# First feed-forward block: the snapshot of one product in PSUM, half of a low part on VectorE, and a fixed order of products

## The chip, the cores and the metric

The kernel runs on one core of one Trainium2 chip. The metric is the device time of one execution in microseconds. Three executions of the kernel before took 986.99, 991.24 and 991.29 us, so the median is 991.24 us. A separate execution was profiled; it took 986.47 us, and its profiled span is 984.5 us.

## The reference

One inference step of a decoder trunk of depth one: 512 prompt tokens and 8 single sample tokens go through the same weights, with model width 1024. In short form:

```python
def _swiglu(x, wg, wu, wd):
    return (jax.nn.silu(x @ wg) * (x @ wu)) @ wd

h = h + 0.5 * _swiglu(_rms_norm(h, ffn1_norm), ffn1_w_gate, ffn1_w_up, ffn1_w_down)   # FFN_DIM = 2816
h = h + mixer(_rms_norm(h, mix_norm))       # pooling mixer and SSD (state space) mixer, states written out
h = h + 0.5 * _swiglu(_rms_norm(h, ffn2_norm), ffn2_w_gate, ffn2_w_up, ffn2_w_down)
y = _rms_norm(h, final_norm)
```

All of it is float32, and the outputs are `y` for prompt and samples and the new states of the mixer. The change touches the first feed-forward block only (gate, up and a part of the down projection).

## The kernel before

Activations lie with features on the 128 partitions and the 520 tokens along the free axis, in two halves of 260. Every large product is done with split operands: a weight or activation `w` is kept as a high part (`hi`, `w` rounded to the matmul's input type) and a low part (`lo = w - hi`), and `mm3` (lines 132 to 137) makes three matmuls of 128x128 by 128x260 from them: hi by hi (L133), hi weight by lo activation (L136), lo weight by hi activation (L137).

In the first block (`Ffn` with `i == 1`) the gate and up weights of one of 22 blocks of 128 hidden features are taken together as a two by two problem: seven products replace eight (a Winograd form of Strassen's scheme). One such group is called a tile here. The first two blocks (0 and 1) are done plainly while the input arrives; tiles 2 to 21 follow in `stream` (L494), and after tile 8 and after tile 16 come four tiles named `Down(c, d)` each, which do the down projection of the eight hidden blocks before in the same seven product form. That makes 20 + 8 tiles of 7 products of 12 matmuls. The rest of the down projection is done by `down` in plain form.

The seven products of a tile are numbered 1 to 7 in `product` (L431). They go to three PSUM banks: bank `A` takes products 1, 6, 7 and 4 one after the other, added up; the pair of banks `BE` takes product 2 in its first bank, and products 5 and then 3, added up, in its second. Since bank A (and the second of BE) hold intermediate sums that are needed on their own, ScalarE copies them out with L456: after product 1 to `a[:,0]`, after 6 to `a[:,1]`, after 7 to `c[:,0]`, after 5 to `c[:,1]`. The next product into that bank can only begin when the copy is done. There are two tiles of `A` and two of `BE`, so that two tiles of work overlap.

`gates` (L460) then adds `BE` and `a` on VectorE (L473), multiplies by the normalisation (L474), applies Silu on ScalarE (L475) and multiplies half of it by `c` (L476). `close` (L478) runs once product 4 is in bank A: it multiplies the other half (L488) and calls `keep_g` (L317), which for every second tile makes the sums and the high and low parts of the gated activations (`gs`).

The weights of a tile go through these steps. `load` (L355) brings the raw weights (two transfers of 512 KB from SP's queue, L366) into one of two `raw` pairs. The unit named `a` (`whi`, `wlo`; used by products 1 and 2) is the first raw half: its high part is a ScalarE cast (L218); its low part is made by `part_by_dma` (L217): ScalarE writes `-hi` (L219), and a transfer issued by GpSimd (L220) adds the raw weights to it from memory. There are two buffers of `whi` and `wlo` in this block, so `whi` of tile t+2 needs product 2 of tile t to be finished. `sums` (L376) makes two sums on VectorE (`s1` by L396, `s2` by L397 and L398) and splits them into the units `c` (products 5 and 7) and `d` (products 6 and 3): cast on ScalarE (L121), low part on VectorE (L123), two buffers. `quarter` (L414) makes the unit `b` (`qhi`, `qlo`, one buffer, product 4) in the way of `part_by_dma`, 512 columns wide; for the `Down` tiles and tile 21 its low part is made on VectorE (L224). The cast `qhi` of tile t needs product 4 of tile t-1 finished, for there is one buffer. It is also the last reader of the raw pair, so the load of tile t+2 waits for it.

The order of instructions on each engine is not the program's: a planner with a model of durations picks, for each engine, what is ready first, with the order of the program as the priority. `pin=True` in `mm3` calls `keep_in_program_order`, which ties a product's first matmul behind the matmul written before it; before, only two products are pinned. `queued(x)` ties instructions behind `x` on the same engine. `stream` writes the products of tile t as 1(t), 4(t-1), then 5, 6, 3, 7, 2 of t (for tiles 2 and 21: 2, 5, 6, 3, 7), but in the trace TensorE mostly runs 1(t), 5(t), 4(t-1), 6, 3, 2, 7.

Of the kernel before, what the change touches and what calls it, by code (L numbers as in the profile page):

```python
# [10 lines left out]
F32 = mybir.dt.float32  # L11
F32R = mybir.dt.float32r
AF = mybir.ActivationFunctionType
ALU = mybir.AluOpType
# [8 lines left out]
HB = NT // 2  # L23
HALVES = (slice(0, HB), slice(HB, NT))
KD = D // P
FFN = 2816
KF = FFN // P
# [36 lines left out]
def tile_trunk_step(ctx: ExitStack, tc: tile.TileContext, ins: dict, outs: dict):  # L64
    nc = tc.nc
# [26 lines left out]
    def queued(*ins):  # L92
        stack = ExitStack()
        for i in ins:
            stack.enter_context(tc.issue_after(i))
        return stack

    def raw_pair(name):
        return wp.tile([P, 2, 1024], F32, tag="raw", bufs=2, name=f"raw_{name}")
# [39 lines left out]
    def ws(w, k, m=P):  # L139
        return w[:, k * m : (k + 1) * m]  # L140
# [76 lines left out]
    def part_by_dma(hi, lo, s, home):  # L217
        nc.scalar.copy(hi, s)  # L218
        nc.scalar.activation(out=lo, in_=hi.bitcast(F32), func=AF.Copy, scale=-1.0)  # L219
        nc.gpsimd.dma_start(out=lo, in_=home, accum_op=ALU.add)  # L220
# [22 lines left out]
    class Ffn:  # L243
# [4 lines left out]
        def __init__(self, nx, i, wx, gp, direct):  # L248
            self.nx, self.i, self.wx, self.gp, self.direct = nx, i, wx, gp, direct
            self.states = None  # L250
            self.folded = CHUNKS[0] + CHUNKS[1] if i == 1 else 0
            self.held = {} if self.folded else {CHUNKS[0] + 1: None, CHUNKS[0] + CHUNKS[1] + 1: None}
            self.dram, self.gs, self.pairs, self.few, self.later = {}, {}, {}, [], []
            self.w, self.A, self.BE, self.ac, self.g, self.tg, self.raw, self.banks, self.behind, self.plain_kept = (
                {} for _ in range(10)
            )
# [98 lines left out]
        def load(self, f, first, then, by_dma):  # L355
            i, wx, src = self.i, self.wx, ins[f"w{self.i}gu"]
            n = f"{i}_{f}"
            raw = raw_pair(n)
            if isinstance(f, int):
                drams = [src[2 * f + u] for u in range(2)]  # L360
            else:
                lo = f.c * CHUNKS[0]
                drams = [ins[f"w{i}d"][2 * f.d + u, :, lo * P : (lo + 8) * P] for u in range(2)]
            self.dram[f] = drams
            for u in range(2):
                nc.sync.dma_start(out=raw[:, u], in_=drams[u])  # L366
            with queued(*first):
                if self.folded and (f, 0) not in LOW_ON_DVE:
                    d1 = weight_homes(1024, f"{n}a", wp, 3, ("whi", "wlo"))
                    part_by_dma(*d1, raw[:, 0], drams[0])  # L370
                else:
                    d1 = split(raw[:, 0], 1024, f"{n}a", wp, 3, ("whi", "wlo"))
            with queued(*then, *(ends if by_dma and i == 1 else ())):
                self.sums(f, n, src, raw, d1, by_dma)
# [56 lines left out]
        def product(self, f, p):  # L431
            js = range(KD // 2)
            if f not in self.A:
                self.load(f, *self.behind.get(f, ((), (), False)))
                n = f"{self.i}_{f}"
                self.A[f] = ps[0].tile([P, 512], F32, tag="A", bufs=2, name=f"A{n}")
                self.BE[f] = ps[0].tile([P, 2, 512], F32, tag="BE", bufs=2, name=f"BE{n}")
                self.ac[f] = [self.wx.tile([P, 2, HB], F32, tag="ac", bufs=3, name=f"ac{n}_{q}") for q in range(2)]
            if p != 1 and 4 not in self.w[f]:
                self.quarter(f, self.held[f])  # L440
            slot, dst, opens = {1: (0, 0, True), 2: (1, 1, True), 5: (3, 2, True), 6: (5, 0, False),
                                3: (2, 2, False), 7: (4, 0, False), 4: (6, 0, False)}[p]
            out = self.A[f] if dst == 0 else self.BE[f][:, dst - 1]
            (whi, wlo), k = self.w[f][p]
            xth, xtl = self.nx[:2]
            for j in js:
                if isinstance(f, int):
                    x = xth[:, j, slot], xtl[:, j, slot]
                else:
                    x = (self.gs[f.c * CHUNKS[0] // 2 + j][:, q, {5: 6, 6: 5}.get(slot, slot)] for q in range(2))  # L450
                mm3(out[:, :HB], ws(whi, k[j]), ws(wlo, k[j]), *x, opens and j == 0,
                    j == KD // 2 - 1, pin=j == 0 and (f, p) in ((2, 7), (3, 1)), skip_group_check=True)
            a, c = self.ac[f]
            keep = {1: a[:, 0], 6: a[:, 1], 7: c[:, 0], 5: c[:, 1]}.get(p)
            if keep is not None:
                nc.scalar.copy(keep, out[:, :HB])  # L456
            if p == 7:
                nc.vector.tensor_tensor(out=c[:, 0], in0=c[:, 0], in1=c[:, 1], op=ALU.add)

        def gates(self, f):  # L460
            if not isinstance(f, int):
                td = self.nx[2].rearrange("p (b t) -> p b t", b=2)
                r = self.nx[3].rearrange("p (b t) -> p b t", b=2)
                hd = h[:, 2 * f.d].rearrange("p (b t) -> p b t", b=2)
                a, c = self.ac[f]
                nc.vector.tensor_tensor(out=td, in0=self.BE[f][:, :, :HB], in1=a, op=ALU.add)
                nc.vector.scalar_tensor_tensor(out=td, in0=td, scalar=-0.5, in1=r, op0=ALU.mult, op1=ALU.mult)
                nc.vector.tensor_tensor(out=hd, in0=td, in1=hd, op=ALU.add)
                nc.vector.scalar_tensor_tensor(out=c[:, 1], in0=c[:, 0], scalar=0.5, in1=r[:, 1], op0=ALU.mult,
                                               op1=ALU.mult)  # L470
                return
            tg = self.tg[f] = self.gate_home(f)
            nc.vector.tensor_tensor(out=tg, in0=self.BE[f][:, :, :HB], in1=self.ac[f][0], op=ALU.add)  # L473
            nc.vector.tensor_tensor(out=tg, in0=tg, in1=self.nx[3].rearrange("p (b t) -> p b t", b=2), op=ALU.mult)  # L474
            nc.scalar.activation(out=tg, in_=tg, func=AF.Silu)  # L475
            nc.vector.tensor_tensor(out=tg[:, 1], in0=self.ac[f][1][:, 0], in1=tg[:, 1], op=ALU.mult)  # L476

        def close(self, f):  # L478
            if not isinstance(f, int):
                r = self.nx[3].rearrange("p (b t) -> p b t", b=2)  # L480
                hd = h[:, 2 * f.d + 1].rearrange("p (b t) -> p b t", b=2)
                c = self.ac[f][1]
                nc.vector.scalar_tensor_tensor(out=c[:, 0], in0=self.A[f][:, :HB], scalar=0.5, in1=r[:, 0],
                                               op0=ALU.mult, op1=ALU.mult)
                nc.vector.tensor_tensor(out=hd, in0=c, in1=hd, op=ALU.add)
                return
            tg = self.tg[f]
            nc.vector.tensor_tensor(out=tg[:, 0], in0=self.A[f][:, :HB], in1=tg[:, 0], op=ALU.mult)  # L488
            self.keep_g(f, tg)
# [4 lines left out]
        def stream(self, before, last_chunk):  # L494
            tiles = []
            for f in range(self.direct, KF):
                tiles.append(f)
                if f and f <= self.folded and f % CHUNKS[0] == 0:
                    tiles.extend(Down(f // CHUNKS[0] - 1, d) for d in range(KD // 2))
            prev = None  # L500
            for t in tiles:
                self.product(t, 1)
                if prev is not None:
                    self.product(prev, 4)
                    self.close(prev)
                for p in (2, 5, 6, 3, 7) if t in (2, KF - 1) else (5, 6, 3, 7, 2):
                    self.product(t, p)
                self.gates(t)
                if t == 3:
                    with queued(*ends[1:]):  # L510
                        self.later.pop()()
                prev = t
            self.product(KF - 1, 4)
            with tc.high_priority():
                self.close(KF - 1)
            before()
            self.down(len(CHUNKS) - 1, self.folded, KF, last_chunk)
# [143 lines left out]
    ffn1 = Ffn(nx1, 1, wx1, g1, 2)  # L661
    xg1, late = [], []
    room = [*ffn1.cells("x2"), *ffn1.cells("x1"), *ffn1.cells("x0")]
    spare = [t.bitcast(F32) for t in ffn1.cells("sq")]
    sqs = spare.pop().rearrange("p (a b) t -> p a (b t)", a=2)
    ffn1.pairs[2] = spare.pop()

    def cell1(name):
        return room.pop().bitcast(F32)
# [723 lines left out]
```

## Time and profile before

| quantity | value |
|---|---|
| median of three executions | 991.24 us (986.99 to 991.29) |
| profiled execution, its own time | 986.47 us |
| its span | 984.5 us |
| TensorE matmuls busy | 966.0 us, 98% |
| VectorE busy | 815.6 us, 83% |
| ScalarE busy | 605.4 us, 61% |
| GpSimd (issue of transfers) busy | 125.7 us, 13% |
| stretch in which the seven product tiles run | about 34 to 335 us |

How to read it: busy time is the union of the instructions' spans. Matmuls overlap in the array: a matmul row lasts about 0.28 us, but one starts every 0.12 us when nothing waits, so the spacing of starts and the idle time before a matmul say more than busy time. In rows of time order the columns are start and duration in us, engine, line, operation, output <- inputs, shapes, count, and in brackets the idle time of the engine before it with what ended that. In rows of groups the columns after the bar are busy us, mean ns of one, and idle us before them with what ended it. Rows of stretches give for PE (matmul), PEld (weight load), DVE (VectorE), ACT (ScalarE) and POOL (GpSimd) the busy us and the instruction count, then the granted clock, the share of the DMA engines' time and GB/s.

### The profile page before, as it was taken

The numbers are of one execution on the slowest core, as the hardware profiler recorded it, in microseconds if no ns is written. First come the engines' busy times: TensorE is split into PE (matmuls) and PEld (weight loads), VectorE is DVE, ScalarE is ACT, GpSimd is POOL, SyncE is SP. The second block draws the span as 40 slices with busy tenths as digits, with TensorE's granted clock in tenths as the row PEclk, the third lists the DMA queues.
The fourth block names the chain that finished last, engine by engine and source line by source line (L and its number), as shares of the span: only waits on it lengthen the run. The fifth ranks groups of instructions, "written<-read, shape, count | busy, mean of one in ns | idle before, by whom it ended". The sixth has DMA issues, their size and how long they took to land.

```text
span 984.5 us, 19586 instructions
## 1 busy us (share of the span) xinstructions
PE 966.0 (98%) x7772; PEld 944.8 (96%) x7772; DVE 815.6 (83%) x1340; ACT 605.4 (61%) x1112; POOL 125.7 (13%) x206
## 2 busy tenths in 40 slices
PE   9999999999999999999999999999999999999996
PEld 8899999999989999999999999999999999999995
DVE  6898987888877688879978897999967899667886
ACT  7778657777557465485776675666643566514663
POOL 0011101111111000056341000100012000110010
PEclk9999999999999999999999999999999999999998
DMA  7577666776567232253334232523346423462232
GB/s 208 162 187 175 150 169 164 169 196 150 133 175 175 97 124 87 92 195 129 108 139 158 73 137 87 154 101 129 115 119 187 160 89 126 123 176 80 86 119 87
DMA packets 50459, 135.18 MB, mean 137 GB/s; under 512 B 7288, under 2 KB 15416, under 8 KB 50368
## 3 DMA queue, kind: packets, MB, share of 16 engines
q1 hardware_dynamic: 39840, 104.18, 30.8%
q0 software_dynamic: 10256, 29.63, 15.7%
q8 instruction: 61, 1.00, 0.4%
q14 instruction: 30, 0.25, 0.1%
q10 hardware_dynamic: 272, 0.13, 0.0%
HBM read 126.57 MB, written 7.34 MB: 136 GB/s over the span
## 4 chain that ended last, share of the span: by engine, by line
PE 78%; DVE 7%; DMA 7%; ACT 4%; issue 3%; SPq 0%; DVEq 0%; ACTq 0%
PE A L133 7%; PE A L136 7%; PE A L137 7%; PE BE L137 5%; PE BE L136 5%; PE BE L133 5%; PE P L282 4%; PE dn L137 4%; PE dn L136 4%; PE dn L133 4%; DMA raw<-in_w1gu 4%; PE wo L133 2%; PE wo L137 2%; PE wo L136 2%; PE inx L133 2%
## 5 line engine op out<-in xcount | busy, mean ns | idle before, releaser
L137 PE MATMUL dn<-g,wlo_2d 128*128 128x260 f32 x256 | 72.5, 283 | 0.0
L133 PE MATMUL dn<-g,whi_2d 128*128 128x260 f32 x256 | 72.1, 282 | 0.0
L136 PE MATMUL dn<-g,whi_2d 128*128 128x260 f32 x256 | 72.1, 282 | 0.0
L396 DVE TENSOR_TENSOR s<-raw 128x1024 f32<-128x1024 f32 x39 | 47.6, 1220 | 22.0 <-DMA raw<-in_w1gu 18.8
L456 ACT COPY ac<-A 128x260 f32<-128x260 f32 x123 | 44.0, 372 | 17.7 <-PE A L137 16.9
L133 PEld LDWEIGHTS dn<-g,whi_2d 128*128 128x128 f32 x256 | 48.2, 188 | 0.0
L136 PEld LDWEIGHTS dn<-g,whi_2d 128*128 128x128 f32 x256 | 48.2, 188 | 0.0
L137 PEld LDWEIGHTS dn<-g,wlo_2d 128*128 128x128 f32 x256 | 48.1, 188 | 0.0
L582 DVE SCALAR_TENSOR_TENSOR td<-dn,r_f 128x520 f32<-128x520 f32 (+1 forms) x25 | 16.8, 675 | 32.5 <-PE dn L137 32.5
L1121 POOL DMA_DIRECT2D out_nss<-hs x16 | 8.7, 545 | 259.1 <-DVE hs L1119 259.0
L121 ACT CAST whi_2d<-raw_2d 128x1024 fp32r<-128x1024 f32 (+1 forms) x18 | 18.5, 1026 | 36.8 <-PE dn L136 15.0
L133 PE MATMUL wo<-catg,whi_wo 128*128 128x260 f32 x128 | 37.1, 290 | 0.0
L133 PE MATMUL inz<-xh_mx,whi_inz 128*128 128x260 f32 x128 | 36.6, 286 | 0.0
L133 PE MATMUL inx<-xh_mx,whi_inx 128*128 128x260 f32 x128 | 36.4, 284 | 0.0
L137 PE MATMUL wo<-catg,wlo_wo 128*128 128x260 f32 x128 | 36.3, 283 | 0.0
L136 PE MATMUL inz<-xl_mx,whi_inz 128*128 128x260 f32 x128 | 36.2, 283 | 0.0
L137 PE MATMUL inz<-xh_mx,wlo_inz 128*128 128x260 f32 x128 | 36.2, 283 | 0.0
L136 PE MATMUL inx<-xl_mx,whi_inx 128*128 128x260 f32 x128 | 36.1, 282 | 0.0
L137 PE MATMUL inx<-xh_mx,wlo_inx 128*128 128x260 f32 x128 | 36.1, 282 | 0.0
L136 PE MATMUL wo<-catg,whi_wo 128*128 128x260 f32 x128 | 36.1, 282 | 0.0
L968 DVE SCALAR_TENSOR_TENSOR A<-U,h,A 128x544 f32<-128x544 f32 x36 | 28.8, 801 | 2.2 <-ACT A L966 1.8
L1117 ACT ACTIVATE so<-br,sxdt 128x128 f32<-128x128 f32 x64 | 20.4, 391 | 16.3 <-DMA br<-scr_bc 9.6
(2135 smaller groups left out, 4384.1 us busy)
## 6 DMA issues: line engine op xcount, KB each, us to landing
raw<-in_w2gu SPq DMA_DIRECT2D x44, 512.0 KB, 4.4
raw<-in_w1gu SPq DMA_DIRECT2D x41, 512.0 KB, 5.4
raw_2d<-in_w2d SPq DMA_DIRECT2D x16, 512.0 KB, 4.6
raw_wo<-in_w_out SPq DMA_DIRECT2D x12, 512.0 KB, 4.4
ab<-scr_acs SPq DMA_DIRECT2D x8, 512.0 KB, 3.7
h<-in_state_ssm SPq DMA_DIRECT2D x16, 256.0 KB, 3.2
raw_inz<-in_w_in SPq DMA_DIRECT2D x8, 512.0 KB, 4.4
hs<-in_state_ssm POOLq DMA_DIRECT2D x16, 256.0 KB, 3.4
```

The lines of the kernel that those rows point to most:

```text
L121: cast = nc.scalar.copy(h, src)
L133: first = nc.tensor.matmul(ps, whi, xhi, start=start, stop=False, **kw)
L136: nc.tensor.matmul(ps, whi, xlo, start=False, stop=False, **kw)
L137: nc.tensor.matmul(ps, wlo, xhi, start=False, stop=stop, **kw)
L282: mm = nc.tensor.matmul(self.banks[f, u][b][:, :HB], ws(self.raw[f][:, u], j + 4 * q), xg[:, slot[q]], start=j == q == 0, stop=j == 3 and ...
L396: nc.vector.tensor_tensor(out=s1, in0=diag, in1=up0, op=ALU.add)
L456: nc.scalar.copy(keep, out[:, :HB])
L582: nc.vector.scalar_tensor_tensor(out=o, in0=s, scalar=-0.5, in1=q, op0=ALU.mult, op1=ALU.mult)
L968: nc.vector.scalar_tensor_tensor(out=A[:, :n], in0=U[:, j : j + n], scalar=w(j), in1=A[:, :n], op0=ALU.mult, op1=ALU.add)
L1117: nc.scalar.activation(out=o[:, q], in_=br, func=AF.Copy, scale=sxdt[:, j, b : b + 1]))
L1121: tc.keep_in_program_order(nc.gpsimd.dma_start(out=outs["nss"][:, b, 4 * g : 4 * g + 4], in_=hs))
```

## The change

- In the first block, except for tile 2 (`whole`), the copy after product 1 goes to the first bank of `BE` in PSUM instead of to SBUF, and product 2 adds to it instead of opening the bank. The sum in `gates` (new method `sum`) then covers only the second bank, 260 columns instead of 520, and is written in place in PSUM; the multiplication by the normalisation reads `BE`.
- For tiles 4 to 21 the low part `wlo` of unit `a` is made in two ways: columns 512 to 1023 as before by `-hi` on ScalarE and an adding transfer (now 256 KB), columns 0 to 511 by a subtraction on VectorE. The `Down` tiles keep the whole of it by transfer. The quarter's low parts stay as they were.
- All products of the first block's tiles are pinned, so TensorE runs them in the program's order.
- Silu and the multiplication after it move from `gates` to `close` (new method `silu`), tied behind the last copy made, and `close` of the tile before moves behind the first of the five later products. The delayed `keep_g` of block 1 moves from tile 3 to tile 5, and tile 4's gate home gets a buffer of its own.

The second block uses the same methods and keeps its operations.

```diff
@@ __init__
+            self.whole = (2,)
@@ load
-                    part_by_dma(*d1, raw[:, 0], drams[0])
+                    hi, lo = d1
+                    n2 = 512 if isinstance(f, int) else 0
+                    nc.scalar.copy(hi, raw[:, 0])
+                    nc.scalar.activation(out=lo[:, n2:], in_=hi[:, n2:].bitcast(F32), func=AF.Copy, scale=-1.0)
+                    nc.gpsimd.dma_start(out=lo[:, n2:], in_=drams[0][:, n2:], accum_op=ALU.add)
+                    if n2:
+                        nc.vector.tensor_tensor(out=lo[:, :n2], in0=raw[:, 0, :n2], in1=hi[:, :n2].bitcast(F32), op=ALU.subtract)
@@ product
+            opens = opens and (p != 2 or self.i == 2 or f in self.whole)
-                    j == KD // 2 - 1, pin=j == 0 and (f, p) in ((2, 7), (3, 1)), skip_group_check=True)
+                    j == KD // 2 - 1, pin=j == 0 and ((f, p) in ((2, 7), (3, 1)) or self.i == 1), skip_group_check=True)
             a, c = self.ac[f]
+            if p == 1 and self.i == 1 and f not in self.whole:
+                a = self.BE[f][:, :, :HB]
             keep = {1: a[:, 0], 6: a[:, 1], 7: c[:, 0], 5: c[:, 1]}.get(p)
             if keep is not None:
-                nc.scalar.copy(keep, out[:, :HB])
+                self.copied = nc.scalar.copy(keep, out[:, :HB]).ins
@@ new methods
+        def sum(self, f, home=None):
+            be, a = self.BE[f][:, :, :HB], self.ac[f][0]
+            if self.i == 2:
+                nc.vector.tensor_tensor(out=home, in0=be, in1=a, op=ALU.add)
+                return home
+            s = slice(0, 2) if f in self.whole else slice(1, 2)
+            nc.vector.tensor_tensor(out=be[:, s], in0=be[:, s], in1=a[:, s], op=ALU.add)
+            return be
+        def silu(self, f):
+            tg = self.tg[f]
+            with queued(*(() if self.i == 2 else (self.copied,))):
+                nc.scalar.activation(out=tg, in_=tg, func=AF.Silu)
             nc.vector.tensor_tensor(out=tg[:, 1], in0=self.ac[f][1][:, 0], in1=tg[:, 1], op=ALU.mult)
@@ gates (the form for Down tiles uses be = self.sum(f) likewise)
-            nc.vector.tensor_tensor(out=tg, in0=self.BE[f][:, :, :HB], in1=self.ac[f][0], op=ALU.add)
-            nc.vector.tensor_tensor(out=tg, in0=tg, in1=self.nx[3].rearrange("p (b t) -> p b t", b=2), op=ALU.mult)
-            nc.scalar.activation(out=tg, in_=tg, func=AF.Silu)
+            nc.vector.tensor_tensor(out=tg, in0=self.sum(f, tg), in1=self.nx[3].rearrange("p (b t) -> p b t", b=2), op=ALU.mult)
+            if self.i == 2:
+                self.silu(f)
@@ close
+            if self.i == 1:
+                self.silu(f)
@@ stream
-                    self.close(prev)
-                for p in (2, 5, 6, 3, 7) if t in (2, KF - 1) else (5, 6, 3, 7, 2):
+                for k, p in enumerate((2, 5, 6, 3, 7) if t in (2, KF - 1) else (5, 6, 3, 7, 2)):
+                    if k == 1 and prev is not None:
+                        self.close(prev)
                     self.product(t, p)
-                if t == 3:
+                if t == 5:
@@ before the stream
-    ffn1.pairs[2] = spare.pop()
+    ffn1.pairs[2], ffn1.pairs[4] = spare
```

More of the change, by code (lines that the diff above doesn't have):

```diff
@@ L465, in gates @@
                 a, c = self.ac[f]
-                nc.vector.tensor_tensor(out=td, in0=self.BE[f][:, :, :HB], in1=a, op=ALU.add)
-                nc.vector.scalar_tensor_tensor(out=td, in0=td, scalar=-0.5, in1=r, op0=ALU.mult, op1=ALU.mult)
+                be = self.sum(f)
+                nc.vector.scalar_tensor_tensor(out=td, in0=be, scalar=-0.5, in1=r, op0=ALU.mult, op1=ALU.mult)
                 nc.vector.tensor_tensor(out=hd, in0=td, in1=hd, op=ALU.add)
```

## The prediction

> **What bounds the kernel now.** I read the page first (shares, then the chain that ended last), then the waits of TensorE, then stretches of the first block, then the rows around its longest waits.
>
> ```profile
> span 984.5 us, 19586 instructions
> PE 966.0 (98%) x7772; PEld 944.8 (96%) x7772; DVE 815.6 (83%) x1340; ACT 605.4 (61%) x1112; POOL 125.7 (13%) x206
> ...
> PE 78%; DVE 7%; DMA 7%; ACT 4%; issue 3%; SPq 0%; DVEq 0%; ACTq 0%
> ```
> ```profile
> PE A L133 <- ACT ac L456: 4.9, 3, 2.4
> PE A_Down(c=1, d=1)_2849 L133 <- ACT ac_Down(c=1, d=1)_1_2852 L456: 1.2, 1, 1.2
> ...
> PE A_Down(c=0, d=1)_1314 L133 <- ACT ac_Down(c=0, d=1)_1_1317 L456: 0.5, 1, 0.5
> PE A_Down(c=1, d=2)_2973 L133 <- ACT ac_Down(c=1, d=2)_1_2976 L456: 0.3, 1, 0.3
> ```
> ```profile
> 85.00:95.00 10.00, 10.00 (x85) 10.00 (x84) 8.47 (x13) 6.86 (x12) 1.68 (x2) 1.00 0.81 184
> 275.00:300.00 25.00, 22.61 (x174) 22.27 (x173) 17.25 (x25) 16.72 (x26) 3.35 (x4) 0.93 0.64 160
> 42.00:325.00 283.00, 275.40 (x2239) 271.80 (x2238) 236.09 (x346) 195.31 (x305) 36.90 (x44) 0.99 0.67 162
> 292.00:294.00 2.00, 2.00 (x11) 2.00 (x11) 2.00 (x6) 1.31 (x4) 0.40 (x1) 0.50 1.05 215
> ```
>
> The reader is to see that TensorE is the bound, and that no matmul is added or removed by the change, so all there is to win is TensorE's lost time inside the seven product tiles. From 42 to 325 us it is idle 283.0 - 275.4 = 7.6 us, and 6.9 us of it (4.9 + 1.2 + 0.5 + 0.3) is a matmul into bank A that waits for a ScalarE copy. A good stretch starts a matmul every 10.0 / 85 = 0.118 us. The stretch from 275 us also shows a granted clock of 0.93, which is 25 x 0.07 = 1.7 us lost, at half clock from 292 us, just after the longest wait. Now how such a wait comes about (tile 9 and 10; ScalarE, the load, TensorE):
>
> ```profile
> 152.71 0.85 SPq L366 DMA_DIRECT2D raw<-in_w1gu  x2
> 155.22 1.05 ACT L121 CAST shi_10c<-s 128x1024 fp32r<-128x1024 f32 x1 [0.69 <-PE BE L136]
> 159.42 1.05 ACT L218 CAST whi_11a<-raw 128x1024 fp32r<-128x1024 f32 x1 [3.15 <-DMA raw<-in_w1gu]
> 160.50 1.06 ACT L219 ACTIVATE wlo_11a<-whi_11a 128x1024 fp32r<-128x1024 f32 x1
> 161.47 1.03 ACT L121 CAST shi_10d<-s 128x1024 fp32r<-128x1024 f32 x1
> 162.40 0.64 ACT L456 COPY ac<-A 128x260 f32<-128x260 f32 x2
> 286.96 1.05 ACT L218 CAST whi_19a<-raw 128x1024 fp32r<-128x1024 f32 x1 [3.79 <-DMA raw<-in_w1gu]
> ```
> ```profile
> 155.14 0.28 PE L133 MATMUL BE<-xth_f,whi_9a 128*128 128x260 f32 x1
> 156.57 0.28 PE L133 MATMUL A<-xth_f,shi_9c 128*128 128x260 f32 x1
> 158.03 0.28 PE L133 MATMUL A<-xth_f,whi_10a 128*128 128x260 f32 x1
> 159.47 0.28 PE L133 MATMUL BE<-xth_f,shi_10c 128*128 128x260 f32 x1
> 162.82 0.39 PE L133 MATMUL A<-xth_f,qhi_9b 128*128 128x260 f32 x1 [1.75 <-ACT ac L456]
> 290.36 0.39 PE L133 MATMUL A<-xth_f,qhi_17b 128*128 128x260 f32 x1 [2.39 <-ACT ac L456]
> ```
>
> TensorE runs 2(9) at 155.14, 7(9) at 156.57, 1(10), 5(10), then 4(9). ScalarE is a queue in order: it has the cast `whi_11a` ahead of the copy that 4(9) needs, and that cast stands 3.15 us for its raw weights, whose load was issued at 152.71. The copy comes at 162.4 although 7(9) ended near 158.2. The same happens at 287 us.
>
> **The change part by part.**
>
> *Fixed order.* Two things in it act on this wait. First, 7 now comes before 2. The planner can place `whi` of tile t+2 only behind product 2 of tile t (two buffers), so the copy after 7 is ready one product earlier than that cast and goes ahead of it in ScalarE's queue. Second, 4(t-1) follows 1(t) directly, without 5(t) between, 12 x 0.119 = 1.43 us sooner. `qhi`, the release of the raw pair and the load on SP's queue all move up by that, while the end of 2(t) moves 1.4 us back: the 3.15 us wait becomes about 0.3 us. That takes the cause from the 6.9 us of idle. Each such wait also costs 0.11 us in its first matmul (0.39 against 0.28), about 0.8 us over the seven or so.
>
> What is late next: the quarter's transfer.
>
> ```profile
> 91.25 0.83 POOL L220 DMA_DIRECT2D qlo_7b<-in_w1gu  x1 [3.70 <-ACT qlo_7b L219]
> 98.48 0.28 PE L137 MATMUL A<-xth_f,qlo_7b 128*128 128x260 f32 x1
> qlo_7b<-in_w1gu POOLq DMA_DIRECT2D x1, 256.0 KB, 6.4
> qlo_9b<-in_w1gu POOLq DMA_DIRECT2D x1, 256.0 KB, 8.2
> qlo_17b<-in_w1gu POOLq DMA_DIRECT2D x1, 256.0 KB, 8.3
> ```
>
> From issue to first use there are 98.48 - 91.25 = 7.23 us; 6.4 fits, 8.2 and 8.3 would be 1.0 us late, in tiles 9 and 17. That loop (4(t-1), cast, negation, transfer, 4(t)) moves as a whole, so its slack stays. Half of the other adding transfer is gone, which takes load off; I leave 1.0 us of the 2.0 for it.
>
> *Copies with less room.* After 6 comes 3 and then 7 at once, so the copy of bank A has one product, 1.43 us, where before 2(t) lay between as well. The same holds for 5 and 3. A copy takes 0.37 us (rows below); behind a cast of 1.05 just begun it ends 1.42 after the product: on the edge. Between 0 and 0.6 us a tile (bound under the rivals); I take 0, because `whi` and both `shi` casts wait for ends of 2, 3 and 7, and so cannot stand in front of these two copies when on time.
>
> *The halves of the low part, and the sum.*
>
> ```profile
> L397 DVE TENSOR_TENSOR s<-s,raw 128x512 f32<-128x512 f32 x19 | 13.0, 683 | 0.0
> L473 DVE TENSOR_TENSOR gq<-BE,ac 128x520 f32<-128x520 f32 x17 | 11.8, 695 | 0.6
> L474 DVE TENSOR_TENSOR gq<-gq,r_f 128x520 f32<-128x520 f32 x17 | 11.8, 693 | 0.0
> L488 DVE TENSOR_TENSOR gq<-A,gq 128x260 f32<-128x260 f32 x16 | 6.7, 420 | 0.3 <-PE A L137 0.3
> L396 DVE TENSOR_TENSOR s<-raw 128x1024 f32<-128x1024 f32 x18 | 22.0, 1223 | 19.4 <-DMA raw<-in_w1gu 18.8 <-DVE slo_13c L123 0.6
> ```
> ```profile
> L456 ACT COPY ac<-A 128x260 f32<-128x260 f32 x56 | 19.2, 371 | 2.8 <-PE A L137 2.8
> L219 ACT ACTIVATE wlo_7a<-whi_7a 128x1024 fp32r<-128x1024 f32 x1 | 1.1, 1062 | 0.0
> L219 ACT ACTIVATE qlo_5b<-qhi_5b 128x512 fp32r<-128x512 f32 x1 | 0.6, 631 | 0.0
> ```
>
> VectorE gains a subtraction of 512 columns (0.68 us) in 18 tiles and gives back 0.695 - 0.42 = 0.27 us in the sum, net +0.41 us a tile, 7.4 us in all. It is busy 8.47 of 10 us in a good stretch, so it goes to about 8.9 of 10: covered while it isn't held up, and its largest hold-up (18.8 us for raw weights) shrinks with the earlier loads. ScalarE gives back 1.06 - 0.63 = 0.43 us a tile. The subtraction delivers the columns of product 1 a whole tile ahead; the transfer's half is only for product 2. All this lies beside TensorE: 0 on the path, at worst the full 7.4.
>
> The multiplication now reads PSUM and the sum writes it. The rows say 0.695 us with a PSUM input and 0.693 without, so I take no difference. The Trainium skill (Perfetto Trace Analysis, Optimizing Scalar/DVE Operations) speaks against the change here: it gives VectorE about 60 ns of access overhead on SBUF and 125 on PSUM. By that, as an estimate, VectorE's load would grow by another 0.07 us a tile; these rows do not show it.
>
> *Snapshot into PSUM.* ScalarE's copy of 0.37 us only changes its target; no row shows a copy into PSUM, and I bound it by 0 to 0.1 us either way, hidden in the two products before 6. *Silu later, `close` later, delayed `keep_g`, own buffer for tile 4:* they order work that has a tile's time; at the start they take four VectorE and three ScalarE steps out of tiles 3 and 4. I count 0 for these.
>
> *Clock.* The half-speed stretch follows the 2.39 us stall; without the stall I take its 1.7 us as gone. The Trainium skill (TensorE: Matmul & The Clock Gate, What's actually happening) has the clock halved after an idle window of about 3.4 us, longer than this stall; by that alone the 1.7 us would stay and the sum be 6.7. The trace puts the slow stretch right behind the stall.
>
> **The sum:** idle -6.9, restarts -0.8, clock -1.7, quarter +1.0: -8.4 us. On the profiled execution's own 986.47 us (span 984.5 and 2.0 around it) that gives 978.1. The median of the runs shown, 991.24, stands 4.8 us above that execution, and one run (986.99) stands beside it; I take the middle, 988.9, as the base: 980.5 us. Bounds: all idle and clock won on the low base, 986.5 - 7.6 - 0.8 - 1.7 = 976; on the high base with half of the win, 987.
>
> **Rivals.**
> - *The wait moves on (no change).* Quarter transfers, tied one behind the other with the new halves, come 0.3 us late in most tiles: 20 x 0.3 = 6 us given back, 988.9 - 8.4 + 6 = 986.5, up to 990. For it: 7.23 against 6.4 leaves 0.8 us only. Against: the loop keeps its length and the traffic falls.
> - *Copies late (slower).* The rows below show 7(6) ending at 85.59 + 0.29 = 85.88 and two copies, its own among them, done at 87.89, 2.0 us later.
>
> ```profile
> 86.31 1.03 ACT L121 CAST shi_7d<-s 128x1024 fp32r<-128x1024 f32 x1
> 87.25 0.64 ACT L456 COPY ac<-A 128x260 f32<-128x260 f32 x2
> 85.59 0.29 PE L137 MATMUL A<-xth_f,slo_6c 128*128 128x260 f32 x1
> ```
>   With 1.43 us of room each tile then loses 0.6 us at 6 to 7: 27 x 0.6 = 16, so 996.5 us. It turns the sign from 0.31 us a tile on. Against: ScalarE has 31% of idle in 85 to 95 us.
> - *VectorE becomes the bound (slower).* If its idle time can't shrink, 18 x 0.41 = 7.4 us come on top and nothing is won: 996 to 998. Against: it is idle 1.5 of 10 us.
>
> **How the numbers follow.** Forecast, 975 to 987: 0.62. The wait moves on: 0.18. Copies late: 0.11. VectorE bound: 0.07. Others: 0.02. A measurement of this kernel tells about 0.5%, 5 us, from no change: faster (under 986.3) 0.62, same 0.19, slower (over 996.2) 0.19. The range 974 to 996 leaves out about 2 in 10; the likeliest case's own is 975 to 987.
>
> **What would show it.** Right: the wait of A for the copy nearly gone from TensorE's waits, `whi` casts waiting for raw under 1 us, clock 1.00 from 275 to 300, idle under 2 us from 42 to 325. Wrong: waits of A or BE for copies repeated in every tile, first uses of `qlo` that wait for its transfer, or VectorE near 10 of 10 us. The likeliest error is in what the planner does with ScalarE's queue, which the trace of before can't show.

## The result, and the profile after

The changed kernel takes 983.3 us (median of 20 runs, 980.48 to 988.49) against 988.62 us for the kernel before (20 runs, 986.56 to 991.64): a ratio of 0.9951, 95% interval 0.9937 to 0.9964. Measured again beside the last experiments (f0 below) it was 0.9925 (0.991 to 0.994). So it is faster by 5.3 us where the forecast had 8.4 us less than 988.9, and the gain is about as large as the 0.5% that was called the least to be told from no change. The profiled span went from 984.5 to 980.0 us.

First the page after, busy times and the shares of the chain that ended last.

```profile
span 980.0 us, 19596 instructions
PE 963.4 (98%) x7772; PEld 943.0 (96%) x7772; DVE 818.4 (84%) x1358; ACT 602.3 (61%) x1112; POOL 125.1 (13%) x206
...
PE 74%; issue 9%; DMA 6%; DVE 5%; ACT 4%; POOL 1%; SPq 0%; DVEq 0%; POOLq 0%; ACTq 0%
```

The gain lies wholly in the first block. The first matmul of `psr_mx`, which comes after that block, starts 4.5 us earlier, as much as the span is shorter (time order, the kernel before, then after):

```profile
369.01 0.60 PE L182 MATMUL psr_mx<-acc_mx,ones 128*128 128x260 f32 x2
```
```profile
364.54 0.60 PE L182 MATMUL psr_mx<-acc_mx,ones 128*128 128x260 f32 x2
```

The same stretches as before, after the change:

```profile
85.00:95.00 10.00, 10.00 (x85) 9.96 (x84) 9.38 (x16) 7.46 (x13) 1.68 (x2) 1.00 0.59 139
275.00:300.00 25.00, 24.43 (x199) 23.89 (x198) 21.81 (x34) 17.41 (x30) 4.83 (x6) 1.00 0.61 141
42.00:325.00 283.00, 277.43 (x2280) 274.48 (x2278) 240.80 (x367) 194.79 (x309) 36.90 (x44) 1.00 0.61 152
```

TensorE's idle time from 42 to 325 us fell from 7.6 to 283.0 - 277.43 = 5.6 us only, and the clock from 275 us is 1.00 instead of 0.93. Idle time -2.0 and clock -1.7 make -3.7 of the -4.5 us. The last 0.8 us has no row of its own: a matmul lasts 0.28 us and one starts every 0.118, so the first 0.16 us of every gap is covered by the matmul before and isn't counted as idle. The count of matmuls in the stretch says the same without this flaw: 2280 - 2239 = 41 more in the same 283 us, 41 x 0.118 = 4.8 us.

What TensorE waits for in the first block now (total, times, longest):

```profile
PE A L137 <- DMA qlo_10b<-in_w1gu: 1.3, 1, 1.3
PE BE_Down(c=1, d=2)_2986 L133 <- ACT BE_Down(c=1, d=2)_2986 L466: 0.9, 1, 0.9
PE A L137 <- DMA qlo_14b<-in_w1gu: 0.9, 1, 0.9
PE A L133 <- ACT ac L466: 0.6, 1, 0.6
PE A L137 <- DMA qlo_18b<-in_w1gu: 0.5, 1, 0.5
PE BE L133 <- ACT BE L466: 0.4, 1, 0.4
PE A L137 <- DMA qlo_7b<-in_w1gu: 0.4, 1, 0.4
PE A L137 <- DMA qlo_8b<-in_w1gu: 0.4, 1, 0.4
```

The names have changed. Waits for a ScalarE copy went from 6.9 us to 0.9 + 0.6 + 0.4 = 1.9. Five waits for the adding transfer of a quarter's low part, none of which stood in the list of before, make 1.3 + 0.9 + 0.5 + 0.4 + 0.4 = 3.5 us. Of 5.0 us won, 3.5 went to the next in the row. These are sums of one profiled execution: in a second profile of the same kernel (f0) five quarters are late by 1.9 us together, and copies by 1.7. Bank A's 0.6 us is the wait of tile 2 at 45.4 us, which was there before with 0.7 us. The waits of `BE` are new: product 5 waits there for the copy of product 1 into the other bank of the pair.

The place that the prediction worked out, tile 9 and 10, after the change (time order; ScalarE, then TensorE):

```profile
156.19 1.05 ACT L121 CAST shi_10d<-s 128x1024 fp32r<-128x1024 f32 x1 [0.40 <-PE A L136]
157.15 0.36 ACT L466 COPY ac<-A 128x260 f32<-128x260 f32 x1
157.64 1.05 ACT L373 CAST whi_11a<-raw 128x1024 fp32r<-128x1024 f32 x1
154.67 0.28 PE L133 MATMUL A<-xth_f,shi_9c 128*128 128x260 f32 x1
156.12 0.28 PE L133 MATMUL BE<-xth_f,whi_9a 128*128 128x260 f32 x1
171.15 0.39 PE L137 MATMUL A<-xth_f,qlo_10b 128*128 128x260 f32 x1 [1.26 <-DMA qlo_10b<-in_w1gu]
```

7(9) starts at 154.67 and 2(9) at 156.12. The copy after 7(9) runs at 157.15, ahead of the cast `whi_11a`, and that cast no longer stands for its raw weights. The last row is the longest of the new waits.

Why the quarter's transfer is late is seen on GpSimd, which issues both adding transfers. One row of the kernel before (its partner, `qlo_7b` at 91.25, stands in the prediction), then after:

```profile
86.71 0.84 POOL L220 DMA_DIRECT2D wlo_8a<-in_w1gu  x1 [4.75 <-ACT wlo_8a L219]
```
```profile
88.13 0.84 POOL L375 DMA_DIRECT2D wlo_8a<-in_w1gu  x1 [8.00 <-PE A L137]
89.40 0.84 POOL L220 DMA_DIRECT2D qlo_7b<-in_w1gu  x1 [0.43 <-ACT qlo_7b L219]
```

In this place the transfer of `wlo` for tile t+2 was issued 91.25 - 86.71 = 4.5 us ahead of the quarter's before, and 1.3 us ahead now. That is the closest pair of the run: over tiles 3 to 20 without 8 and 16 the median distance went from 4.2 to 2.4 us, and after the change it lies between 1.3 and 3.2. The cast `whi` of tile t+2 waits for the end of 2(t), the cast `qhi` of tile t+1 for the end of 4(t). Between those two products stood 7(t), 1(t+1) and 5(t+1), so the ends were four products of 1.43 us apart, 5.7; the fixed order leaves only 1(t+1) between them, two products, 2.9 us. With the smaller distance the quarter's transfer takes longer (transfers of after: bytes each, us from issue to landing):

```profile
wlo_8a<-in_w1gu POOLq DMA_DIRECT2D x1, 256.0 KB, 7.6
qlo_7b<-in_w1gu POOLq DMA_DIRECT2D x1, 256.0 KB, 7.7
qlo_10b<-in_w1gu POOLq DMA_DIRECT2D x1, 256.0 KB, 8.7
```

Over the 18 quarter transfers of a run, worked out from these rows: median 6.45 us before, two over 7.2; median 7.20 after, eight over 7.2. The room from issue to first use (tiles 4 to 20 without 9 and 17, which begin behind the `Down` tiles) has a median of 7.39 us before and 7.28 after. What did not move is the raw load: SP issues it 0.93 us ahead of the quarter's transfer in nearly every tile, before and after (rows for `qlo_7b`, before, then after):

```profile
90.31 0.80 SPq L366 DMA_DIRECT2D raw_Down(c=0, d=0)_1166<-in_w1d  x2
```
```profile
88.47 0.80 SPq L367 DMA_DIRECT2D raw_Down(c=0, d=0)_1168<-in_w1d  x2
```

The distance does not explain every late quarter. `qlo_10b`, the slowest, was issued 2.8 us behind its partner:

```profile
159.64 0.84 POOL L375 DMA_DIRECT2D wlo_11a<-in_w1gu  x1 [7.15 <-ACT BE L466]
162.45 0.83 POOL L220 DMA_DIRECT2D qlo_10b<-in_w1gu  x1 [1.97 <-DVE wlo_11a L377]
```

That partner landed after 4.2 us, so 1.3 us behind the quarter's issue, hardly later than in most tiles before the change (1.0 to 1.3 us). The same holds for `qlo_14b` and `qlo_18b`; these three make 2.7 of the 3.5 us, and why they were slow stays open. Over many transfers the distance does show. In the five profiles that keep this issue order (after, e5, e9, f0, f2; 80 quarters, without tiles 8 and 16) the median latency is 7.5 us where the distance was under 2.0 us, 7.2 from 2.0 to 2.6, and 6.2 above that.

### The profile page after: what moved, and what is told of

Same layout as the page of the kernel before. It is cut to its first block, busy times and chain, and to the rows that moved or that the text cites. A ratio compares the mean times of both kernels' runs of the same rounds, so it can differ in the third digit from the quotient of the medians.

```text
span 980.0 us, 19596 instructions
## 1 busy us (share of the span) xinstructions
PE 963.4 (98%) x7772; PEld 943.0 (96%) x7772; DVE 818.4 (84%) x1358; ACT 602.3 (61%) x1112; POOL 125.1 (13%) x206
## 4 chain that ended last, share of the span: by engine, by line
PE 74%; issue 9%; DMA 6%; DVE 5%; ACT 4%; POOL 1%; SPq 0%; DVEq 0%; POOLq 0%; ACTq 0%
PE A L137 6%; PE A L133 6%; PE A L136 6%; PE P L283 4%; PE BE L137 4%; PE BE L136 4%; PE dn L137 4%; PE dn L136 4%; PE BE L133 4%; PE dn L133 4%; DMA raw<-in_w1gu 2%; PE wo L133 2%; PE wo L137 2%; PE wo L136 2%; PE inx L133 2%
## 5 line engine op out<-in xcount | busy, mean ns | idle before, releaser
L466 ACT COPY ac<-A 128x260 f32<-128x260 f32 x104 | 38.4, 372 | 30.5 <-PE A L137 29.6
```

Source lines behind the costliest of these rows:

```text
L466: self.copied = nc.scalar.copy(keep, out[:, :HB]).ins
```

## The experiments

Two theories stood against each other. **Q**: the order removed the copy waits as predicted, and the rest of the gain is lost to the quarter's transfer, because the other adding transfer is now issued close ahead of it. **The rival**: something else that the change brings eats it (VectorE near its limit, the snapshot in PSUM, Silu moved into `close`). Beside them stood the question which part of the change earns the gain. Ratios are against the kernel before, run beside each on the same chip; "idle" is TensorE's from 42 to 325 us of the profiled execution; "latency" is the median from issue to landing of the quarter transfers, worked out from their rows. All kernels compute the whole of the reference.

| run | median us | ratio (95%) | idle us | latency us, how many of 18 over 7.2 |
|---|---|---|---|---|
| before | 988.62 to 991.72 | 1 | 7.6 | 6.45, 2 |
| changed | 983.3 | 0.9951 (0.9937 to 0.9964) | 5.6 | 7.20, 8 |
| e1_half_behind_quarter | 978.45 | 0.9889 (0.9871 to 0.9906) | 2.8 | 6.85, 3 |
| e2_order_only | 991.19 | 1.0013 (0.9998 to 1.0028) | 11.3 | 7.25, 9 |
| e3_no_order | 991.21 | 1.0017 (1.0004 to 1.003) | 10.9 | 6.30, 1 |
| e4_low_whole | 990.97 | 1.0016 (1.0005 to 1.0027) | 11.5 | 7.60, 11 |
| e5_no_snapshot | 980.84 | 0.9898 (0.9865 to 0.9931) | 4.8 | 7.15, 6 |
| e6_quarter_vector | 979.33 | 0.9879 (0.9855 to 0.9904) | 3.5 | none |
| e8_low_vector | 981.61 | 0.9905 (0.9879 to 0.9932) | 4.8 | 5.85, 2 |
| e9_silu_as_before | 982.48 | 0.992 (0.989 to 0.995) | 6.9 | 7.30, 10 |
| f0_changed_again | 981.86 | 0.9925 (0.991 to 0.994) | 4.6 | 7.20, 9 |
| f1_half_behind_again | 977.77 | 0.9889 (0.9871 to 0.9906) | 3.5 | 6.70, 4 |
| f2_no_snapshot_again | 983.1 | 0.9933 (0.9911 to 0.9955) | 7.0 | 7.20, 8 |
| f3_behind_no_snapshot | 976.99 | 0.9869 (0.9854 to 0.9884) | 1.75 | 6.65, 1 |

e1 to e4 ran on one chip (the kernel before took 989.43 us there), e5, e6, e8 and e9 on a second (991.72), f0 to f3 on a third (990.27). On the second chip the changed kernel itself was not measured, so those four are compared with it only through their ratios.

**The other transfer behind the quarter's.** Only the order of two issues on GpSimd is changed.

```diff
@@ part_by_dma
-        nc.gpsimd.dma_start(out=lo, in_=home, accum_op=ALU.add)
+        return nc.gpsimd.dma_start(out=lo, in_=home, accum_op=ALU.add).ins
@@ __init__
+            self.lastq = ()
@@ load
-                    nc.gpsimd.dma_start(out=lo[:, n2:], in_=drams[0][:, n2:], accum_op=ALU.add)
+                    with queued(*self.lastq if n2 else ()):
+                        nc.gpsimd.dma_start(out=lo[:, n2:], in_=drams[0][:, n2:], accum_op=ALU.add)
@@ quarter
-                    part_by_dma(h, l, src, home)
+                    self.lastq = (part_by_dma(h, l, src, home),)
```

> The changed kernel with one difference: GpSimd issues the half transfer of the low part of tile t+1 behind the quarter's transfer of tile t. Theory Q (the quarter's transfer is late because the half transfer is issued 1.3 to 2.4 us ahead of it and shares the DMA engines): the quarter's transfers fall from 7 to 8.7 us to 6.0 to 6.6 us as before the change, the waits of matmuls for them (4 to 5 us in the changed kernel) go under 1 us, and the time is 3 to 5 us below the changed kernel, near 979. Rival V (VectorE's higher load, or the raw load, slows the quarter's transfer): transfers stay at 7 to 8 us and the time near 983.

The issue order turned round and the latency fell; GpSimd's rows, TensorE's waits for the quarter, the same transfer as above, and the stretch:

```profile
90.93 0.84 POOL L220 DMA_DIRECT2D qlo_7b<-in_w1gu  x1 [8.81 <-ACT qlo_7b L219]
91.47 1.17 POOL L377 DMA_DIRECT2D wlo_8a<-in_w1gu  x1
```
```profile
PE A L137 <- DMA qlo_4b<-in_w1gu: 0.7, 1, 0.7
PE A L137 <- DMA qlo_7b<-in_w1gu: 0.7, 1, 0.7
```
```profile
qlo_10b<-in_w1gu POOLq DMA_DIRECT2D x1, 256.0 KB, 6.6
```
```profile
42.00:325.00 283.00, 280.22 (x2316) 278.32 (x2316) 242.68 (x372) 195.97 (x311) 37.38 (x44) 1.00 0.61 153
```

`qlo_10b` takes 6.6 us where it took 8.7, idle time falls from 5.6 to 2.8 us, and the stretch holds 2316 matmuls against 2280. The half of `wlo` that now goes second has its time: its first use comes a product tile later. It needs that time: it takes 7.6 us now (median of its transfers), where it took 3.8 in front. So whichever of the two goes second is slowed, which follows Q. In size Q had asked for more: 6.0 to 6.6 us for the quarters and waits under 1 us, where the median is 6.85, two quarters take 8.0, and the waits are 1.4 us. It was run again with the changed kernel beside it:

> The changed kernel once more, as the measure for the three beside it on the same chip: a ratio to the kernel before of 0.993 to 0.996.

> The kernel with the half transfer issued behind the quarter's, again: theory Q says 0.987 to 0.991 of the kernel before, and clear of the changed kernel.

0.9925 (0.991 to 0.994), a little under what was expected, and 0.9889 (0.9871 to 0.9906): the order of these two issues is worth about 981.86 - 977.77 = 4.1 us, with intervals that only just part. The two profiled executions (981.18 and 979.34 us) differ by less, and the waits for quarters in them are 1.9 and 1.1 us, so not all of the 4.1 us is seen as such a wait.

**The order alone.** The kernel before, with the new pins.

```diff
@@ product, of the kernel before
-                    j == KD // 2 - 1, pin=j == 0 and (f, p) in ((2, 7), (3, 1)), skip_group_check=True)
+                    j == KD // 2 - 1, pin=j == 0 and ((f, p) in ((2, 7), (3, 1)) or self.i == 1), skip_group_check=True)
```

> The kernel before with all products of the first block pinned in the program's order, and nothing else of the change. If the order alone carries the gain: waits of bank A for the copy nearly gone and 981 to 985 us. If it needs the halved transfer beside it (theory Q): the whole 512 KB transfer now comes 2 us ahead of the quarter's, the quarter takes 8 us or more as in tiles 9 and 17 before, a wait of about 1 us in most tiles, 988 to 1000 us.

No gain: 1.0013 (0.9998 to 1.0028), and a median latency of 7.25 us, where 8 or more was expected. TensorE's waits, the longest:

```profile
PE A L137 <- DMA wlo_16a<-in_w1gu: 2.2, 1, 2.2
PE A L137 <- DMA qlo_17b<-in_w1gu: 1.5, 1, 1.5
PE A L137 <- DMA qlo_9b<-in_w1gu: 1.3, 1, 1.3
PE A L133 <- ACT ac L456: 1.1, 1, 1.1
```

The copy waits shrink here too (3.0 us in all), and transfers take their place: the quarter's (4.1 us), and the undivided `wlo` (3.7 us), which the order moved nearer to its first use. What the order wins at the copies it loses here, until the transfer is halved.

**The changed kernel without the order**, and **with the order, but all of `wlo` by transfer**.

```diff
@@ product, of the changed kernel (e3)
-                    j == KD // 2 - 1, pin=j == 0 and ((f, p) in ((2, 7), (3, 1)) or self.i == 1), skip_group_check=True)
+                    j == KD // 2 - 1, pin=j == 0 and (f, p) in ((2, 7), (3, 1)), skip_group_check=True)
@@ load, of the changed kernel (e4)
-                    n2 = 512 if isinstance(f, int) else 0
+                    n2 = 0
```

> The changed kernel without the new pins: the planner orders TensorE as it did before. If the order carries the gain: waits of bank A for the copy after 7 are back with several us, and the time is 986 to 990 us. If the lighter engines carry it: 983 us or less.

> The changed kernel with the whole low part of unit a by the adding transfer again (512 KB, no half on VectorE). Theory Q: the quarter's transfer behind a transfer of twice the size takes 8 to 9 us, 1 to 2 us late in most of 16 tiles, 990 to 1000 us. Rival V (VectorE's load is what costs): 980 us or less, since VectorE gets 0.68 us a tile back.

Both lose the whole gain (1.0017 and 1.0016; the first is a little slower than expected). TensorE's waits without the order, then with the undivided transfer:

```profile
PE A L133 <- ACT ac L466: 5.8, 10, 1.1
PE A_Down(c=1, d=1)_2861 L133 <- ACT ac_Down(c=1, d=1)_1_2864 L466: 1.7, 1, 1.7
```
```profile
PE A L137 <- DMA wlo_16a<-in_w1gu: 1.8, 1, 1.8
PE A L137 <- DMA qlo_17b<-in_w1gu: 1.4, 1, 1.4
```

Without the order the copy waits are back, each shorter but more of them, 10.7 us in all where the kernel before had 6.9. The quarter's transfer is quick (6.30 us), with the same half transfer 4.2 us ahead of it instead of 2.4. With the undivided transfer it is the slowest of all (7.60 us), and `wlo` itself comes late, by 4.1 us over four tiles: with the halves no wait for `wlo` is listed. So the order earns nothing by itself (e2), nor does the rest of the change without it (e3) or without the halves (e4): the halves and the order need each other. The halves alone, without anything else, were not run.

**No low part of `a` by transfer**, and **no quarter by transfer**: VectorE makes them.

```diff
@@ load (e8)
-                    n2 = 512 if isinstance(f, int) else 0
+                    n2 = 1024 if isinstance(f, int) else 0
...
-                    nc.scalar.activation(out=lo[:, n2:], in_=hi[:, n2:].bitcast(F32), func=AF.Copy, scale=-1.0)
-                    nc.gpsimd.dma_start(out=lo[:, n2:], in_=drams[0][:, n2:], accum_op=ALU.add)
+                    if n2 < 1024:
+                        nc.scalar.activation(out=lo[:, n2:], in_=hi[:, n2:].bitcast(F32), func=AF.Copy, scale=-1.0)
+                        nc.gpsimd.dma_start(out=lo[:, n2:], in_=drams[0][:, n2:], accum_op=ALU.add)
@@ quarter (e6)
-                if isinstance(f, int) and (f, 1) not in LOW_ON_DVE:
+                if False:
```

> The changed kernel with the whole low part of unit a by VectorE in tiles 4 to 21 (1024 columns, 1.22 us) and no adding transfer for it. Theory Q: the quarter's transfer has no transfer ahead of it and takes 6.0 to 6.5 us, its waits vanish. Rival V: VectorE gets 0.54 us a tile more, near 10 of 10 us, and TensorE waits for its low parts: 985 us or more. Which of the two is larger is told by the time against 983.

> The changed kernel with every quarter's low part made by VectorE (one subtraction of 512 columns, 0.68 us a tile) and no quarter transfer. Theory Q alone: the waits for the quarter's transfer vanish, 978 to 980 us. Rival V (VectorE as the bound): its load goes from 9.4 to about 10 of 10 us, waits of matmuls for VectorE's low parts appear, 985 to 995 us.

With 0, 256 and 512 KB of `wlo` in a tile the quarter's transfer takes 5.85 (e8), 7.20 (changed) and 7.60 us (e4): Q in three steps. The only two over 7.2 us in e8, 7.7 and 7.3, are tiles 8 and 16, which still have the whole `wlo` transfer of a `Down` tile 2.0 and 2.4 us ahead. VectorE's price shows as well. First the kernel without the transfer of `wlo`, a row of TensorE:

```profile
82.40 0.39 PE L137 MATMUL A<-xth_f,slo_6d 128*128 128x260 f32 x1 [2.81 <-DVE slo_6d L123]
```

Then the kernel with every quarter on VectorE, TensorE's longest wait and the stretch from 85 us:

```profile
PE A L137 <- DVE slo_6d L123: 2.1, 1, 2.1
```
```profile
85.00:95.00 10.00, 10.00 (x85) 10.00 (x85) 10.00 (x18) 6.73 (x12) 0.83 (x1) 1.00 0.35 75
```

VectorE is busy 10.00 of 10 us there, and TensorE still starts its 85 matmuls. It is late once, for `slo_6d`, and the kernel is faster than the changed one all the same (0.9879, 0.9855 to 0.9904). So VectorE at its limit did not bound the tile here, and it did not eat the gain. For e8 (0.9905, 0.9879 to 0.9932) the time does not tell whether the transfer saved or VectorE's lateness is the larger: its interval overlaps that of the changed kernel beside f1.

**The snapshot, and the place of Silu.**

```diff
@@ __init__ (e5)
-            self.whole = (2,)
+            self.whole = (*range(KF), *(Down(c, d) for c in range(2) for d in range(KD // 2)))
@@ gates, close, stream (e9)
-            if self.i == 2:
-                self.silu(f)
+            self.silu(f)
...
-            with queued(*(() if self.i == 2 else (self.copied,))):
-                nc.scalar.activation(out=tg, in_=tg, func=AF.Silu)
+            nc.scalar.activation(out=tg, in_=tg, func=AF.Silu)
...
-            if self.i == 1:
-                self.silu(f)
...
-                for k, p in enumerate((2, 5, 6, 3, 7) if t in (2, KF - 1) else (5, 6, 3, 7, 2)):
-                    if k == 1 and prev is not None:
-                        self.close(prev)
+                    self.close(prev)
+                for p in (2, 5, 6, 3, 7) if t in (2, KF - 1) else (5, 6, 3, 7, 2):
```

> The changed kernel with the copy after product 1 in SBUF again, product 2 opening its bank and the sum over both banks (520 columns), for all tiles. As predicted, the snapshot is worth nothing on the path: the time is that of the changed kernel within 1.5 us, near 983. If VectorE's 0.27 us a tile counts (its load is 9.4 of 10 us in a good stretch now): 985 to 990 us.

> The changed kernel with Silu in the gates and the close of the tile before at their old places in the program. As predicted (counted 0): 983 us within 1.5. If Silu ahead of the copies in ScalarE's queue makes the copies after 5 and 6 late, which have one product of room now: waits of BE and A for copies in many tiles, 986 to 995 us.

> The changed kernel without the snapshot, again. If the snapshot is worth nothing: the changed kernel's time within 1.5 us. If its lower time on the other chip (981) was its own and not the chip's: 2 to 4 us below the changed kernel.

Without the snapshot 0.9898 (0.9865 to 0.9931) the first time, 980.84 us and so lower than expected, and 0.9933 (0.9911 to 0.9955) beside the changed kernel's 0.9925: worth nothing that these intervals could show. Silu and `close` at their old places give 0.992 (0.989 to 0.995), which the intervals cannot tell from the changed kernel.

**The best of these together**, the quarter's transfer first and no snapshot (the edits of e1 and e5):

> Both: half transfer behind the quarter's, no snapshot. If the snapshot is worth nothing, the time of the kernel with the half transfer behind, within 1.5 us; if the low time without the snapshot came from the same transfers (their issue shifted), the two gains do not add and the result is the same; if the snapshot itself costs, 2 to 4 us less, near 975.

The fastest kernel of the study, 0.9869 (0.9854 to 0.9884), 13.3 us below the kernel before. All its waits in the first block, and the stretch:

```profile
PE A L137 <- DVE slo_6d L123: 0.9, 1, 0.9
PE A L133 <- ACT ac L468: 0.6, 1, 0.6
```
```profile
42.00:325.00 283.00, 281.25 (x2330) 279.86 (x2329) 249.53 (x372) 195.64 (x311) 37.35 (x44) 1.00 0.60 151
```

Idle is 1.75 us of 283, the least of all. It holds 2330 - 2239 = 91 more matmuls than the kernel before, 91 x 0.118 = 10.7 us, as its span is 984.5 - 973.6 = 10.9 us shorter. That it beats f1 (0.9889) is within the intervals. A second buffer for the quarter, which would cut its loop at the root, was not tried.

## Why the prediction was right, and where a term was off

The sign, the range and the mechanism of the copy waits held; the size was off by more than a third: -5.3 us against -8.4, 983.3 against 980.5. Of its own signs of being right, the waits for copies, the clock and the cast `whi_11a` came as said, but idle time is 5.6 us where it was to be under 2, and three other `whi` casts still wait 1.4 to 1.7 us for raw weights, where under 1 was said. One of its signs of being wrong came true, first uses of `qlo` that wait for their transfer. That the time lies inside the range owes something to its width, 12 us.

- **Base.** 988.9 us was taken for the kernel before; 20 runs gave 988.62. The middle of one low and one high figure came that close by luck.
- **Order and copies, -6.9 us.** As said: the copy went ahead of the cast, `whi_11a` no longer waits for raw weights (3.15 us before), 7 and 2 swapped. But 1.9 us of copy waits stayed, of which 0.9 and 0.4 are the snapshots into `BE`, which were counted at 0: they were taken to be hidden until product 6, and it is product 5 that waits. So -5.0. Bank A keeps 0.6: the wait in tile 2, 0.7 before, which the prediction had counted as won with the others.
- **Clock, -1.7 us.** Came in full in the profiled pair, clock 1.00 from 275 to 300 us. It is a figure of one execution: the mean granted clock of the runs beside each other is 0.9963 before and 0.9968 after (11 runs, and the 6 of f0), which by an estimate is 0.5 us.
- **Restarts, -0.8 us.** Not to be told apart: first matmuls that waited still last 0.38 to 0.39 us, and there are eight of them where there were about seven before. The same 0.8 us is what idle time and clock leave over, but it is not shown to be this term.
- **The quarter's transfer, +1.0 us.** This is the step that failed in size: 3.5 us of listed waits, 1.9 in the second profile. "That loop moves as a whole, so its slack stays" held, 7.39 to 7.28 us of room. "Half of the other adding transfer is gone, which takes load off" did not: the half that stayed was moved to 2.4 us ahead of the quarter's (median), where before the whole of it had 4.2 us of start, and the latency rose from 6.45 to 7.20 us. The prediction followed the order's effect on each loop and not on the distance between the two loops; the four products and the two that set that distance could have been counted in the text's own list of products. e1 turns it round and gets the predicted gain and some more, 978.45 us. What made the three slowest quarters of the profiled execution slow stays open.
- **VectorE, 7.4 us hidden.** Hidden (f0 shows two waits for VectorE, of 0.3 and 0.4 us), and less: +4.7 us from 42 to 325 (236.09 to 240.80). The `Down` tiles' sums got shorter too, 8 x 0.265 = 2.1 us, which the prediction left out. From 85 to 95 us it is busy 9.38, where about 8.9 was expected.
- **Snapshot and PSUM, 0.** The copy into PSUM takes no longer than one into SBUF, nor does a PSUM input slow VectorE. First the copies by their source line in the kernel after (least, median and most ns of one, then first and last start), then its groups on VectorE:

```profile
L466 ACT COPY BE<-A x19: 360/370/382, 46.2 to 316.7; 128x260 f32<-128x260 f32 x19
L466 ACT COPY ac<-A x104: 352/375/384, 36.5 to 934.6; 128x260 f32<-128x260 f32 x104
```
```profile
L476 DVE TENSOR_TENSOR BE<-BE,ac 128x260 f32<-128x260 f32 x19 | 8.2, 430 | 3.9 <-PE BE L137 3.9
L492 DVE TENSOR_TENSOR tg<-tg,r_f 128x520 f32<-128x520 f32 x21 | 14.6, 694 | 0.0
L492 DVE TENSOR_TENSOR gq<-BE,r_f 128x520 f32<-128x520 f32 x16 | 11.1, 693 | 0.0
```

  The medians are 370 ns into PSUM and 375 into SBUF. The multiplication from PSUM takes 693 ns against 694 from SBUF. The Trainium skill (Perfetto Trace Analysis, Optimizing Scalar/DVE Operations) gives VectorE a longer access to PSUM; these rows do not show it.
- **Silu, `close`, `keep_g`, 0.** Nothing measurable for Silu and `close` (e9); `keep_g` was not tried alone.
- **The rivals.** "The wait moves on" was the nearest to what happened: the quarter's transfer did come late, in five tiles by 0.4 to 1.3 us rather than in most by 0.3, and gave back 3.5 us where that rival had 6. "Copies late" did not occur: no wait for a copy repeats by tile. "VectorE bound" did not either, not even at 10.00 of 10 us (e6).

## What to carry to other kernels

When an order of work is fixed, work out for each queue not only how long each loop has, but how far apart its transfers are issued: two transfers that each had enough room were brought together here, and the second became slow. Of two such transfers it paid here to issue the one with the shorter room first, even though the other's data was ready earlier; that one tie was worth about 4 us, nearly as much as the whole change. And parts of a change that are worth nothing one without the other (e2, e3, e4) can be worth half a per cent together, so test each by leaving it out as well as by adding it.

## What the runs showed of the hardware

- An adding transfer of 256 KB has no fixed latency: the fastest `wlo` half of after took 3.6 us, the quarter's 5.85 (median) with no other adding transfer in most tiles (e8), 6.45 with one of 512 KB 4.2 us ahead (before), and 7.2, up to 8.7, with another 1.3 to 3.2 us ahead (after). Put 0.5 us behind the quarter's, the half took 7.6 us (e1).

```profile
wlo_14a<-in_w1gu POOLq DMA_DIRECT2D x1, 256.0 KB, 3.6
```

- Half clock follows a stall less simply than the prediction took it. In the kernel before it came behind a stall of 2.39 us. In e8 a longer one, 2.81 us before the matmul at 82.40, left the clock at full speed (stretch of that kernel):

```profile
82.00:92.00 10.00, 9.60 (x78) 9.47 (x79) 10.00 (x17) 6.57 (x11) 0.00 (x0) 1.00 0.27 76
```

  So a stall's length alone does not decide it. The Trainium skill (TensorE: Matmul & The Clock Gate, What's actually happening) halves the clock after an idle window of about 3.4 us that runs freely; the stall of 2.81 us agrees with that, the one of 2.39 us with half clock behind it does not. Which of them is the exception stays open.
